# Transformer block, gate and up products: other signs, and two of four weight sums by an adding transfer

## The chip, the cores and the metric

The kernel runs on one core of one Trainium2 chip. The time is device microseconds of one execution. Engines are named as in the profile: PE (TensorE; PEld is its weight load), DVE (VectorE), ACT (ScalarE), POOL (GpSimd) and SP (SyncE, which here only issues DMAs).

## The reference

One encoder layer on 1024 positions of width 1024, all in float32. The change lies in the last part, the feed-forward network with 2816 hidden columns:

```
x = x + mix @ w_out                      # mix: convolution heads and neighbourhood attention
h = rms_norm(x, norm2_g)
x = x + (silu(h @ w_gate) * (h @ w_up)) @ w_down
```

## The kernel before

All matrix products are made in float32r with operands split in two: a high part (ACT's cast) and a low part (source minus high part, on DVE or POOL). Each product of tiles is three matmuls (L112 to L114: high by high, high by low, low by high). `split` at L103 does this splitting.

The gate and up products go by a Strassen-Winograd scheme with seven products in place of eight. The hidden columns are cut in 22 blocks of 128 (`FB`); block i has four weight quarters: gate and up, each for the first and second half of the 1024 inputs, named b11 (gate, first half), b21 (gate, second), b12 (up, first), b22 (up, second). The left operands are halves and sums of h, made once (A11, A12, A22, S1 to S4). The seven products of a block, m1 to m7, each take 4 x 3 matmuls of 128x512 and write to three PSUM banks A (m1, m2), B (m6, m5, m3) and D (m7, m4); a bank is accumulated on after DVE or ACT has read what stands in it. The order is m1, m6, m2, m5, m7, m3, m4 (`ORDER`), except that blocks 0 and 1 go through the products side by side.

Weights come by SP in two loads of 512 KB per block (`load_gu`, L874, three buffers `R`). Four weight sums per block are made on DVE (`t_sums`, L882, tiles ts): T1 = b12 - b11, T2 = b22 - T1, T3 = b22 - b12, T4 = b21 - T2. Each of the seven weight tiles (three quarters, four sums) is then split by ACT and POOL to a tile t (t9m in the profile is any of block 9's seven). Tiles ts, t and the results g come from one pool of 22 buffers (`G`).

Two functions set the order, both written out by hand. `product(i, p)` issues the matmuls, `evac(i, p)` the reading of a bank (L1025 to L1047: L1028 for m6, L1033 for m5, L1035 for m7, L1037 for m3, L1041 for m4). After each, `prep` issues the next task: the split of the weight tile of a product that comes four later, with the sums and loads that belong to it (L898 to L926). So sums, splits, evacuations and loads stand in one program order per engine, and each engine works through its own in order. An evacuated block is stored to DRAM (`keep`, L1052, sd), with sums of pairs of blocks on DVE (L1067), for the down projection that follows. While block 0 and 1 run, transposes and splits of the left operands (`s_T`, L946) are woven between their matmuls; S4 is the last of them, split on DVE.

Of the kernel before, what the change touches and what calls it, by code (L numbers as in the profile page):

```python
# [21 lines left out]
FB = FF // P  # L22
# [8 lines left out]
def layout(v):  # L31
    f = {k: np.asarray(a)[0] for k, a in v.items()}
    w_in = f["w_in"]
    ag = w_in[:, :2 * DC].reshape(KB, P, 8, P).transpose(2, 1, 0, 3)
    qkv = w_in[:, 2 * DC:].reshape(4, 2, P, 3, 512).transpose(3, 0, 2, 1, 4)
    gu = np.stack([f["w_gate"], f["w_up"]]).reshape(2, KB, P, FB, P).transpose(3, 0, 2, 1, 4)
    wd = f["w_down"].reshape(FB, P, D)
    par = np.concatenate([
        f["norm1_g"].reshape(KB, P).T,
        f["dw_kernel"].reshape(CW, 4, P).transpose(2, 1, 0).reshape(P, 4 * CW),  # L40
        f["dw_bias"].reshape(4, P).T,
        f["conv_ln_g"].reshape(4, P).T,
        f["conv_ln_b"].reshape(4, P).T,
        np.concatenate([f["q_norm_g"]] * 2)[:, None],
        np.concatenate([f["k_norm_g"]] * 2)[:, None],
    ], axis=1)
    out = {
        "x": f["x"],
        "xt": f["x"].T.reshape(4, 2, P, 2, 512).transpose(3, 0, 2, 1, 4),
        "ag": ag.reshape(8, P, KB * P),  # L50
        "qkv": qkv.reshape(3, 4, P, 1024),
        "wo": f["w_out"],
        "gu": gu.reshape(FB, 2, P, KB * P),
        "wd": wd,
        "g2": f["norm2_g"][None],
        "rpb": f["rpb"],
        "par": par,
    }
    return {k: np.ascontiguousarray(a) for k, a in out.items()}
# [8 lines left out]
def build(ctx, tc, a):  # L68
    nc = tc.nc
    pe, act, dve, pool = nc.tensor, nc.scalar, nc.vector, nc.gpsimd  # L70
# [26 lines left out]
    def tp(name):  # L97
        return ps.tile([P, 512], F32, tag="tp", bufs=2, name=name)

    def cv(name):  # L100
        return ps.tile([P, 1024], F32, tag="cv", bufs=1, name=name)

    def split(hi, lo, src, sub=(pool,)):  # L103
        act.copy(hi, src)  # L104
        n = src.shape[-1] // len(sub)
        for i, eng in enumerate(sub):
            sl = slice(i * n, (i + 1) * n)
            eng.tensor_tensor(*[w[..., sl] for w in (lo, src, hi.bitcast(F32))], OP.subtract)  # L108
# [397 lines left out]
    for kp in range(4):  # L506
# [13 lines left out]
        for j in range(2):  # L520
            for t in range(2):
                k = 2 * kp + j
# [175 lines left out]
    s1 = score_mm(1)  # L698
# [173 lines left out]
    raw_gu, top, tsum = {}, {}, {}  # L872

    def load_gu(i, j):  # L874
        if i < FB:
            raw_gu[i, j] = R(f"gu{i}{j}")
            nc.sync.dma_start(raw_gu[i, j], a["gu"][ms[i], j])

    def lr(w):
        return w[:, :512], w[:, 512:]  # L880

    def t_sums(i, ns):  # L882
        (b11, b21), (b12, b22) = lr(raw_gu[i, 0]), lr(raw_gu[i, 1])
        for n in ns:
            if n in (1, 3):
                tsum[i, n // 2] = G(f"ts{i}{n}")
            o = lr(tsum[i, (n - 1) // 2])[(n - 1) % 2]
            l, r = ((b12, b11), (b22, lr(tsum[i, 0])[0]), (b22, b12), (b21, lr(tsum[i, 0])[1]))[n - 1]
            dve.tensor_tensor(o, l, r, OP.subtract)  # L889


    ORDER = ("m1", "m6", "m2", "m5", "m7", "m3", "m4")
    ms = [m + h * QF for m in range(QF) for h in range(2)]
# [4 lines left out]
    def prep(n=1):  # L898
        for _ in range(n):
            if not tasks:  # L900
                return
            i, p = tasks.pop(0)
            if i < 2:
                if i == 1 and p in ("m6", "m5"):
                    t_sums(i, (1, 2) if p == "m6" else (3, 4))
            elif p == "m1":
                t_sums(i, (1, 2))
            elif p == "m6":
                t_sums(i, (3, 4))
            b = {"m1": (0, 0), "m2": (0, 1), "m3": (1, 1)}.get(p)  # L910
            n = {"m5": 0, "m6": 1, "m7": 2, "m4": 3}.get(p)
            src = lr(raw_gu[i, b[0]])[b[1]] if b else lr(tsum[i, n // 2])[n % 2]
            top[i, p] = lr(G(f"t{i}{p}", F32R))
            split(*top[i, p], src, (dve,) if i < 2 and p in ("m1", "m2", "m6", "m5") else (pool,))
            if (i, p) == (0, "m2"):
                load_gu(1, 1)
            if (i, p) == (1, "m5"):
                load_gu(2, 0)
            if (i, p) == (0, "m3"):
                load_gu(2, 1)  # L920
            if (i, p) == (1, "m3"):
                load_gu(3, 0)
            if i > 1 and p == "m2":
                load_gu(i + 1, 1)
            if i > 1 and p == "m3":
                load_gu(i + 2, 0)  # L926
# [3 lines left out]
    sn, sop = {}, {}  # L930

    def s_sum(t, ns, eng):
        (x11, x12), (x21, x22) = lr(xn[t]), lr(xn[t + 4])
        for n in ns:
            if n == 1:
                sn[t] = G(f"sn{t}")
            s1, s2 = lr(sn[t])
            o, l, r, op = ((s1, x21, x22, OP.add), (s2, s1, x11, OP.subtract),
                           (x21, x11, x21, OP.subtract), (x12, x12, s2, OP.subtract))[n - 1]
            eng.tensor_tensor(o, l, r, op)  # L940

    def s_rows(n, t):
        return {"S1": lambda: sn[t][:, :512], "S2": lambda: sn[t][:, 512:], "S3": lambda: xn[t + 4][:, :512],
# [2 lines left out]
    def s_T(n, kb):  # L946
        if kb == 0:
            if n == "S4":
                q = [lr(G(f"S4{i}", F32R)) for i in range(HK)]
                sop[n] = [[w[h] for w in q] for h in range(2)]  # L950
            else:
                q = H(n, F32R).rearrange("p (w k s) -> p w k s", w=2, s=512)
                sop[n] = [[q[:, h, i] for i in range(HK)] for h in range(2)]
                sop[n, "all"] = [q[:, h] for h in range(2)]
        two = kb == 2
        pt = cv("sp") if two else tp("sq")
        for j in range(1 + two):
            for t in range(4):
                pe.transpose(pt[:, j * 512 + t * P:j * 512 + (t + 1) * P],
                             s_rows(n, t)[:, (kb + j) * P:(kb + j + 1) * P], ident)  # L960
        if two and n != "S4":
            split(*[w[:, kb:kb + 2].rearrange("p k s -> p (k s)") for w in sop[n, "all"]], pt, (dve,))
        else:
            for j in range(1 + two):
                split(sop[n][0][kb + j], sop[n][1][kb + j], lr(pt)[j] if two else pt, (dve,))
# [41 lines left out]
    gt, bank, sl, u2, late = {}, {}, {}, {}, []  # L1007
# [12 lines left out]
    def evac(i, p, acc):  # L1020
        if p == "m1":
            gt[i] = G(f"g{i}")
        l, r = lr(gt[i])
        if p == "m1":
            (act.copy if i else dve.tensor_copy)(l, acc)  # L1025
        elif p == "m6":
            u2[i] = ST(f"u2{i}")
            dve.tensor_tensor(u2[i], acc, l, OP.add)  # L1028
        elif p == "m2":
            sl[i] = ST(f"sl{i}") if i < 2 else acc  # L1030
            act.activation(sl[i], acc, AF.Silu)  # L1031
        elif p == "m5":
            dve.tensor_tensor(r, acc, l, OP.add)  # L1033
        elif p == "m7":
            dve.tensor_tensor(r, acc, r, OP.add)  # L1035
        elif p == "m3":
            dve.tensor_tensor(l, acc, l, OP.add)  # L1037
            dve.tensor_tensor(l, sl[i], l, OP.mult)
            keep(i, 0, l)
        else:  # L1040
            dve.tensor_tensor(acc, acc, u2[i], OP.add)  # L1041
            act.activation(acc, acc, AF.Silu)  # L1042

            def f():
                dve.tensor_tensor(r, acc, r, OP.mult)
                keep(i, 1, r)
            late.append(f)  # L1047
# [165 lines left out]
    for s, p in enumerate(SEQ):  # L1213
        for k in range(QF - 2):
            n = s * QF + k
# [34 lines left out]
```

## Time and profile before

| | us |
|---|---|
| median of 3 runs | 1069.12 (1068.72 to 1070.26) |
| span of the profiled execution | 1067.6 |
| PE busy | 1047.3 (98%) |
| DVE busy | 701.1 (66%) |
| ACT busy | 451.0 (42%) |
| POOL busy | 381.1 (36%) |

The span runs from the first to the last instruction of the profiled execution; the runs' times are of whole executions, 1.1 to 2.7 us longer, and the profiled execution's own time is not listed beside its span. Matmuls overlap, so a matmul of 0.39 us is followed by the next one after 0.23 us. DMA-issuing instructions are not counted as busy on their engines. In the timelines a row is start, us taken, engine, line, operation, output<-inputs, and in brackets the idle time before it and who ended it. The gate and up stage runs from about 420 to 845 us, the down projection from there to the end.

### The profile page before, as it was taken

Reading aid. Unit: us, or ns where it says so; the run is one execution under the profiler, and the core shown is the slowest. Engines: PE = TensorE matmul, PEld = TensorE weight load, DVE = VectorE, ACT = ScalarE, POOL = GpSimd, SP = SyncE. Lnnn points to the kernel's source line nnn. Section 1 sums busy time; section 2 is a strip of 40 time slices with the busy share of each in tenths; the row PEclk is TensorE's granted clock in tenths of the full one; section 3 lists DMA queues with packets and bytes.
Section 4 is the critical chain, followed back from the end, with each engine's and each line's share of the span. In section 5 each row is a group of like instructions: output and inputs, shape, how many; then the busy total and the mean of one; then the engine's idle time right before and its main releaser. Section 6 shows DMA issues by size and latency. Waiting matters only on the chain.

```text
span 1067.6 us, 14069 instructions
## 1 busy us (share of the span) xinstructions
PE 1047.3 (98%) x5068; PEld 848.8 (80%) x5068; DVE 701.1 (66%) x1071; ACT 451.0 (42%) x987; POOL 381.1 (36%) x301
## 2 busy tenths in 40 slices
PE   7999999989999999999999999999999999999997
PEld 5888888866667888788888888888888888888886
DVE  6768997895775346766556465564655567858873
ACT  6465357725775424542322323223232344433441
POOL 0126675513562301445444554445554300002310
PEclk9999999989999999999999999999999999999999
DMA  8416781234414522132322322333232597634641
GB/s 328 167 48 223 218 247 53 75 141 147 152 61 126 163 86 80 41 117 81 128 99 91 128 99 89 109 111 111 74 129 79 184 328 276 207 99 128 206 128 41
DMA packets 68245, 144.06 MB, mean 135 GB/s; under 512 B 12496, under 2 KB 21200, under 8 KB 67536
## 3 DMA queue, kind: packets, MB, share of 16 engines
q1 hardware_dynamic: 66336, 139.95, 39.1%
q10 hardware_dynamic: 1840, 3.22, 0.9%
q8 instruction: 40, 0.66, 0.2%
q14 instruction: 29, 0.24, 0.1%
HBM read 103.99 MB, written 44.76 MB: 139 GB/s over the span
## 4 chain that ended last, share of the span: by engine, by line
PE 94%; DVE 4%; ACT 1%; DMA 0%; issue 0%; SPq 0%; ACTq 0%; DVEq 0%
PE B L114 6%; PE B L112 6%; PE B L113 6%; PE A L112 4%; PE D L114 4%; PE D L112 4%; PE A L114 4%; PE D L113 4%; PE A L113 4%; PE z L112 3%; PE z L113 3%; PE z L114 3%; DVE cv L319 3%; PE gl L114 3%; PE gl L112 3%; PE gl L113 3%
## 5 line engine op out<-in xcount | busy, mean ns | idle before, releaser
L319 DVE SCALAR_TENSOR_TENSOR cv<-u,par,cv 128x1009 f32<-128x1009 f32 (+14 forms) x92 | 117.5, 1277 | 2.5
L345 POOL TENSOR_TENSOR pa<-pa,pr 128x1022 f32<-128x1022 f32 (+5 forms) x24 | 57.5, 2396 | 50.3 <-ACT pr L344 41.9
L104 ACT CAST op<-sr 128x512 fp32r<-128x512 f32 x77 | 47.7, 619 | 51.5 <-PE B2d L114 23.4
L1033 DVE TENSOR_TENSOR g<-B,g 128x512 f32<-128x512 f32 x22 | 15.2, 690 | 78.9 <-PE B L114 78.9
L108 DVE TENSOR_TENSOR op<-sr,op 128x512 fp32r<-128x512 f32 x77 | 56.4, 732 | 16.1 <-ACT op L104 15.8
L1205 POOL TENSOR_TENSOR ou<-ou,resm 128x512 f32<-128x512 f32 x8 | 12.1, 1522 | 144.1 <-DMA resm<-xd 142.2
L1042 ACT ACTIVATE D<-D 128x512 f32<-128x512 f32 x22 | 12.8, 582 | 113.1 <-DVE D L1041 113.1
L1028 DVE TENSOR_TENSOR u<-B,g 128x512 f32<-128x512 f32 x22 | 15.2, 691 | 62.5 <-PE B L114 62.5
L104 ACT CAST op<-wd 128x512 fp32r<-128x512 f32 x66 | 40.9, 620 | 31.4 <-DVE wd L1120 18.1
L633 POOL TENSOR_SCALAR e<-e,rs 128x288 f32<-128x288 f32 (+1 forms) x64 | 34.1, 545 | 51.9 <-DVE rs L631 42.4
L108 DVE TENSOR_TENSOR op<-wd,op 128x512 fp32r<-128x512 f32 x66 | 50.3, 763 | 2.6 <-ACT op L104 1.1
L889 DVE TENSOR_TENSOR ts<-gu,ts 128x512 f32<-128x512 f32 x44 | 51.0, 1159 | 0.8
L1031 ACT ACTIVATE A<-A 128x512 f32<-128x512 f32 x20 | 11.6, 582 | 76.3 <-PE A L114 76.3
L626 ACT ACTIVATE e<-e,mx 128x288 f32<-128x288 f32 (+1 forms) x64 | 36.2, 569 | 11.4 <-DVE mx L624 11.4
L889 DVE TENSOR_TENSOR ts<-gu 128x512 f32<-128x512 f32 x22 | 34.1, 1550 | 0.0
L624 DVE CUSTOM_DVE_ANT_0 e<-s,tab 128x288 f32<-128x288 f32 (+1 forms) x64 | 30.0, 504 | 5.7 <-PE s L611 5.4
L611 PE MATMUL s<-kT,qT 64*128 64x288 f32 (+1 forms) x128 | 28.1, 499 | 4.6 <-DVE mx L624 4.6
L642 PEld LDWEIGHTS p<-ident,e 128*96 128x96 f32 (+1 forms) x192 | 20.1, 133 | 15.0 <-issue 10.4
L372 ACT ACTIVATE sq<-z,r 128x64 f32<-128x64 f32 x96 | 28.6, 334 | 2.2 <-PE z L114 2.2
L642 PE MATMUL p<-ident,e 128*96 128x128 f32 (+1 forms) x192 | 27.6, 280 | 0.6 <-DVE pT L647 0.6
L658 PE MATMUL o<-pT,vw 96*64 96x128 f32 (+1 forms) x384 | 28.0, 281 | 0.0
L344 ACT ACTIVATE pr<-u,par 128x1022 f32<-128x1022 f32 (+5 forms) x24 | 27.0, 1138 | 1.6 <-ACT vs L403 1.6
(1039 smaller groups left out, 3451.4 us busy)
## 6 DMA issues: line engine op xcount, KB each, us to landing
gu<-in_gu SPq DMA_DIRECT2D x44, 512.0 KB
sr<-sd SPq DMA_DIRECT2D x77, 256.0 KB
sd<-sd SPq DMA_DIRECT2D x22, 512.0 KB
wd<-in_wd SPq DMA_DIRECT2D x44, 256.0 KB
sd<-g SPq DMA_DIRECT2D x33, 256.0 KB
x<-in_x SPq DMA_DIRECT2D x16, 512.0 KB
xd<-x SPq DMA_DIRECT2D x8, 512.0 KB
resm<-xd SPq DMA_DIRECT2D x16, 256.0 KB
```

The costliest lines, as they stand in the source:

```text
L104: act.copy(hi, src)
L108: eng.tensor_tensor(*[w[..., sl] for w in (lo, src, hi.bitcast(F32))], OP.subtract)
L112: pe.matmul(acc, lh, rh, start=start, stop=False, skip_group_check=True)
L113: pe.matmul(acc, lh, rl, start=False, stop=False, skip_group_check=True)
L114: pe.matmul(acc, ll, rh, start=False, stop=stop, skip_group_check=True)
L319: dve.scalar_tensor_tensor(acc[:, o], uc[:, i], dwk[:, c, t:t + 1], acc[:, o], OP.mult, OP.add)
L345: pool.tensor_tensor(pa[:, o], pa[:, o], pr[:, o], OP.add)
L624: dve.tensor_tensor_reduce(out=e[:, hh], in0=ss[hh], in1=tab[rh, cb][2 * hp + hh], scale=-1.0, scalar=3.0e38, op0=OP.add, op1=OP.min, accu ...
L626: act.activation(e[:, hh], e[:, hh], AF.Exp, bias=mx, scale=-1.0, accum_out=rs[:, hh:hh + 1])
L633: pool.tensor_scalar(es[i][:, hh], es[i][:, hh], rs[:, hh:hh + 1], 1.0, op0=OP.mult, op1=OP.mult)
L642: pe.transpose(pt[:m, g * P:(g + 1) * P], es[i][:, hh, g * m:(g + 1) * m], ident)
L889: dve.tensor_tensor(o, l, r, OP.subtract)
```

## The change

The signs of the operands are chosen so that all four weight sums are additions: P1 = b11 + b12, P2 = P1 + b22, P3 = b12 + b22, P4 = P2 + b21. The evacuations, the Silu of m4 (scale -1) and the left operands (S1, S2, S3, A22) take the opposite signs where needed. In DRAM the weight quarters are paired anew: the first load of a block is (b11, b22), the second (b12, b21).

For the blocks from 2 on, P1 and P3 lie in one tile of 128x1024 and are no longer made on DVE. `t_first` has SP load b12 into both halves of the tile (two loads of 256 KB), one block ahead, at the split of m1. `t_add` has POOL issue one transfer of 512 KB that adds (b11, b22) from DRAM to the tile, one block ahead, after the split of m7; for block 2 both stand at the splits of m3 of blocks 0 and 1, and for block 3 the loads stand at the split of m1 of block 2. DVE makes P2 at the split of m1 and P4 at the split of m6. Blocks 0 and 1 make all four sums on DVE.

```diff
+    def t_first(i):
+        if i < FB:
+            tsum[i, 0] = G(f"ts{i}0")
+            for j in range(2):
+                nc.sync.dma_start(lr(tsum[i, 0])[j], a["gu"][ms[i], 1][:, :512])
+
+    def t_add(i):
+        if i < FB:
+            pool.dma_start(tsum[i, 0], a["gu"][ms[i], 0], accum_op=OP.add)
+
     def t_sums(i, ns):
-        (b11, b21), (b12, b22) = lr(raw_gu[i, 0]), lr(raw_gu[i, 1])
+        (b11, b22), (b12, b21) = lr(raw_gu[i, 0]), lr(raw_gu[i, 1])
         for n in ns:
-            if n in (1, 3):
-                tsum[i, n // 2] = G(f"ts{i}{n}")
-            o = lr(tsum[i, (n - 1) // 2])[(n - 1) % 2]
-            l, r = ((b12, b11), (b22, lr(tsum[i, 0])[0]), (b22, b12), (b21, lr(tsum[i, 0])[1]))[n - 1]
-            dve.tensor_tensor(o, l, r, OP.subtract)
+            if (n, i < 2) in ((1, True), (2, False)) or n == 2:
+                tsum[i, n - 1] = G(f"ts{i}{n}")
+            if n in (1, 3) and i > 1:
+                continue
+            (p1, p3), (p2, p4) = lr(tsum[i, 0]), lr(tsum[i, 1]) if (i, 1) in tsum else (None, None)
+            o, l, r = ((p1, b11, b12), (p2, p1, b22), (p3, b12, b22), (p4, p2, b21))[n - 1]
+            dve.tensor_tensor(o, l, r, OP.add)
...
             if (i, p) == (0, "m3"):
                 load_gu(2, 1)
+                t_first(2)
             if (i, p) == (1, "m3"):
                 load_gu(3, 0)
+                t_add(2)
+            if i > 1 and p == "m1":
+                t_first(i + 1)
+            if i > 1 and p == "m7":
+                t_add(i + 1)
...
-        if two and n != "S4":
+        if n == "A22":
+            w = slice(kb, kb + 1 + two)
+            hi, lo = [q[:, w].rearrange("p k s -> p (k s)") for q in sop[n, "all"]]
+            act.activation(hi, pt, AF.Copy, scale=-1.0)
+            dve.scalar_tensor_tensor(lo, pt, -1.0, hi.bitcast(F32), OP.mult, OP.subtract)
+        elif two and n != "S4":
...
         elif p == "m6":
             u2[i] = ST(f"u2{i}")
-            dve.tensor_tensor(u2[i], acc, l, OP.add)
+            dve.tensor_tensor(u2[i], acc, l, OP.subtract)
...
             dve.tensor_tensor(acc, acc, u2[i], OP.add)
-            act.activation(acc, acc, AF.Silu)
+            act.activation(acc, acc, AF.Silu, scale=-1.0)
```

DVE in block 9, before. The rows go from the evacuation of m6 to that of m3; ts101 and ts103 are the sums of block 10, gu100 and gu101 its loads, g9 the result, B9 and D9 the banks:

```order
L1028 TENSOR_TENSOR u29_5432<-B9_5419,g9_5413 128x512
L1033 TENSOR_TENSOR g9_5413<-B9_5419,g9_5413 128x512
L889 TENSOR_TENSOR ts101_5468<-gu101_5381,gu100_5301 128x512
L889 TENSOR_TENSOR ts101_5468<-gu101_5381,ts101_5468 128x512
L1035 TENSOR_TENSOR g9_5413<-D9_5474,g9_5413 128x512
L889 TENSOR_TENSOR ts103_5488<-gu101_5381 128x512
L889 TENSOR_TENSOR ts103_5488<-gu100_5301,ts101_5468 128x512
L1037 TENSOR_TENSOR g9_5413<-B9_5419,g9_5413 128x512
```

The same place on DVE in the changed kernel (its lines are numbered anew: L1056 is the evacuation of m5, L1058 of m7, L1060 of m3); ts100 is the tile that the adding transfer fills:

```order
L1051 TENSOR_TENSOR u29_5444<-B9_5431,g9_5424 128x512
L1056 TENSOR_TENSOR g9_5424<-B9_5431,g9_5424 128x512
L902 TENSOR_TENSOR ts102_5480<-ts100_5351,gu100_5312 128x512
L1058 TENSOR_TENSOR g9_5424<-D9_5488,g9_5424 128x512
L902 TENSOR_TENSOR ts102_5480<-ts102_5480,gu101_5392 128x512
L1060 TENSOR_TENSOR g9_5424<-B9_5431,g9_5424 128x512
```

Two sums are gone, and the one ahead of the evacuation of m7 now reads a tile that transfers have filled.

POOL in block 9, before: the splits of m5, m7, m3 and m4.

```order
L108 TENSOR_TENSOR t9m5_5397<-ts91_5335,t9m5_5397 128x512
L108 TENSOR_TENSOR t9m7_5416<-ts93_5357,t9m7_5416 128x512
L108 TENSOR_TENSOR t9m3_5434<-gu91_5241,t9m3_5434 128x512
L108 TENSOR_TENSOR t9m4_5452<-ts93_5357,t9m4_5452 128x512
L108 TENSOR_TENSOR t10m1_5471<-gu100_5301,t10m1_5471 128x512
```

The same place on POOL in the changed kernel:

```order
L109 TENSOR_TENSOR t9m5_5408<-ts90_5212,t9m5_5408 128x512
L109 TENSOR_TENSOR t9m7_5427<-ts90_5212,t9m7_5427 128x512
L891 DMA ts100_5351<-in_gu 128x1024
L109 TENSOR_TENSOR t9m3_5446<-gu90_5176,t9m3_5446 128x512
L109 TENSOR_TENSOR t9m4_5464<-ts92_5346,t9m4_5464 128x512
L109 TENSOR_TENSOR t10m1_5482<-gu100_5312,t10m1_5482 128x512
```

The adding transfer for block 10 (L891) stands between the splits of m7 and m3 of block 9. On SP, where the stage begins, the changed kernel has these rows (gu21 is the second load of block 2, gu30 the first of block 3, L887 the two loads of `t_first`):

```order
L878 DMA gu20_4203<-in_gu 128x1024
L878 DMA gu21_4304<-in_gu 128x1024
L887 DMA ts20_4306<-in_gu 128x512 x2
L878 DMA gu30_4338<-in_gu 128x1024
L887 DMA ts30_4378<-in_gu 128x512 x2
```

Before, the three loads gu20, gu21 and gu30 stood there one behind the other; the loads for the tiles ts20 and ts30 have come between and behind them.

More of the change, by code (lines that the diff above doesn't have):

```diff
@@ L35, in layout @@
     qkv = w_in[:, 2 * DC:].reshape(4, 2, P, 3, 512).transpose(3, 0, 2, 1, 4)
-    gu = np.stack([f["w_gate"], f["w_up"]]).reshape(2, KB, P, FB, P).transpose(3, 0, 2, 1, 4)
+    gu = np.stack([f["w_gate"], f["w_up"]]).reshape(2, 2, KB // 2, P, FB, P).transpose(4, 0, 1, 3, 2, 5)
+    gu = np.stack([np.stack([gu[:, 0, 0], gu[:, 1, 1]], 2), np.stack([gu[:, 1, 0], gu[:, 0, 1]], 2)], 1)
     wd = f["w_down"].reshape(FB, P, D)
@@ L909, in prep @@
                 t_sums(i, (3, 4))
-            b = {"m1": (0, 0), "m2": (0, 1), "m3": (1, 1)}.get(p)
-            n = {"m5": 0, "m6": 1, "m7": 2, "m4": 3}.get(p)
-            src = lr(raw_gu[i, b[0]])[b[1]] if b else lr(tsum[i, n // 2])[n % 2]
+            b = {"m1": (0, 0), "m2": (1, 1), "m3": (0, 1)}.get(p)
+            n = {"m5": (0, 0), "m6": (1, 0), "m7": (0, 1), "m4": (1, 1)}.get(p)
+            src = lr(raw_gu[i, b[0]])[b[1]] if b else lr(tsum[i, n[0]])[n[1]]
             top[i, p] = lr(G(f"t{i}{p}", F32R))
@@ L937, in s_sum @@
             s1, s2 = lr(sn[t])
-            o, l, r, op = ((s1, x21, x22, OP.add), (s2, s1, x11, OP.subtract),
-                           (x21, x11, x21, OP.subtract), (x12, x12, s2, OP.subtract))[n - 1]
-            eng.tensor_tensor(o, l, r, op)
+            o, l, r = ((s1, x21, x22), (s2, x11, s1), (x21, x21, x11), (x12, x12, s2))[n - 1]
+            eng.tensor_tensor(o, l, r, OP.subtract)
     def s_rows(n, t):
@@ L1032, in evac @@
         elif p == "m5":
-            dve.tensor_tensor(r, acc, l, OP.add)
+            dve.tensor_tensor(r, acc, l, OP.subtract)
         elif p == "m7":
@@ L1036, in evac @@
         elif p == "m3":
-            dve.tensor_tensor(l, acc, l, OP.add)
+            dve.tensor_tensor(l, acc, l, OP.subtract)
             dve.tensor_tensor(l, sl[i], l, OP.mult)
```

## The prediction

> **What bounds the kernel now.** I read the page's first two parts, then the table of busy time by stretches, then the waits of PE, and only then the timelines of the engines that the change touches. The page:
>
> ```profile
> span 1067.6 us, 14069 instructions
> PE 1047.3 (98%) x5068; PEld 848.8 (80%) x5068; DVE 701.1 (66%) x1071; ACT 451.0 (42%) x987; POOL 381.1 (36%) x301
> PE 94%; DVE 4%; ACT 1%; DMA 0%; issue 0%; SPq 0%; ACTq 0%; DVEq 0%
> ```
>
> PE is busy for 98% of the span and carries 94% of the chain that ended last. Whether the 98% is even is seen in the stretches (us of the stretch, then PE, PEld, DVE, ACT, POOL busy, granted clock, DMA share, GB/s). Gate and up run from about 420 to 845 us:
>
> ```profile
> 390.00:430.00 40.00, 39.34 (x189) 31.95 (x188) 26.34 (x40) 16.86 (x33) 5.19 (x3) 1.00 0.24 93
> 430.00:470.00 40.00, 39.58 (x212) 32.34 (x212) 28.15 (x40) 20.34 (x34) 17.64 (x14) 1.00 0.12 40
> 470.00:510.00 40.00, 40.00 (x178) 33.13 (x177) 24.56 (x31) 10.52 (x20) 20.23 (x15) 1.00 0.32 112
> ...
> 790.00:830.00 40.00, 40.00 (x178) 33.14 (x177) 23.53 (x29) 11.19 (x21) 20.95 (x16) 1.00 0.27 96
> sum 360.00, PE 360.00 PEld 298.10 DVE 205.87 ACT 103.34 POOL 180.97; mean PE 40.00 PEld 33.12 DVE 22.87 ACT 11.48 POOL 20.11
> ```
>
> From 470 to 830 us PE is busy 360 of 360 us at full clock. In the 80 us before, it lacks 0.66 + 0.42 = 1.1 us. The waits of PE say the same (us in total, times, longest); after 400 us there are two rows:
>
> ```profile
> PE t L990 <- DVE xn L863: 0.6, 1, 0.6
> PE B L113 <- DVE S L108: 0.3, 1, 0.3
> ```
>
> So in the stage that is changed, PE waits for nothing. VectorE is busy only 206 of 360 us there and has no share in the time.
>
> **What is removed.** For the 20 blocks from the third on, two of four sums on DVE go. The groups of the sums, by shape:
>
> ```profile
> L889 DVE TENSOR_TENSOR ts<-gu,gu 128x512 f32<-128x512 f32 x22 | 16.8, 762 | 0.0
> L889 DVE TENSOR_TENSOR ts<-gu 128x512 f32<-128x512 f32 x22 | 34.1, 1550 | 0.0
> ```
>
> 20 x 762 ns + 20 x 1550 ns = 46 us of DVE. PE did not wait for them, so their worth is 0; at most the 1.1 us above could come back, and nothing in it hangs on these sums. The other signs (subtract for add, Silu and Copy with scale -1, the A22 split as one scalar_tensor_tensor) exchange instructions one for one on the same shapes: 0.
>
> **What is added in steady state.** Per block SP issues two more 256 KB loads, and Pool one 512 KB transfer that adds: 20 x 1 MiB = 21 MB beside 144 MB, at a DMA share near 0.3. The question is when the adding transfer lands, because DVE's sum p2 waits for it, and DVE works in order. Take blocks 8 and 9 (tiles t8m, t9m), where the transfers for blocks 9 and 10 are issued. The first line is the page's total, the others are of the timelines of Pool, DVE and PE (start, us taken):
>
> ```profile
> DMA packets 68245, 144.06 MB, mean 135 GB/s; under 512 B 12496, under 2 KB 21200, under 8 KB 67536
> 588.70 1.29 POOL L108 TENSOR_TENSOR t8m<-ts,t8m 128x512 fp32r<-128x512 f32 x1 [0.70 <-ACT t8m L104]
> ...
> 606.38 2.65 POOL L108 TENSOR_TENSOR t9m<-ts,t9m 128x512 fp32r<-128x512 f32 x2 [3.77 <-ACT t9m L104]
> 608.98 1.31 POOL L108 TENSOR_TENSOR t9m<-gu,t9m 128x512 fp32r<-128x512 f32 x1
> 614.79 0.69 DVE L1033 TENSOR_TENSOR g<-B,g 128x512 f32<-128x512 f32 x1 [4.75 <-PE B L114]
> 617.44 0.69 DVE L1035 TENSOR_TENSOR g<-D,g 128x512 f32<-128x512 f32 x1 [0.43 <-PE D L114]
> 600.92 0.39 PE L112 MATMUL D<-A,t8m 128*128 128x512 f32 x1
> ...
> 619.96 0.39 PE L112 MATMUL D<-A,t9m 128*128 128x512 f32 x1
> ```
>
> In block 9 Pool ends the splits of m5 and m7 at 609.03; there the transfer is issued. DVE comes to the sum at 614.79 + 0.69 = 615.5. Queued behind it is L1035, the evacuation of m7, and for that PE waits: m4 accumulates on the same bank D from 619.96. With 0.69 for the sum and 0.69 for L1035, the transfer must land by 619.96 - 1.38 = 618.6, that is 9.5 us after its issue. (In block 8 the split of m7 ends at 588.70 + 1.29 and PE comes to D at 600.92: also 9.5.) A later landing costs PE its lateness once per block, for 19 blocks.
>
> The trace has no Pool transfer and no addition. The nearest rows are two plain transfers of 512 KB from SP:
>
> ```profile
> 591.27 0.33 SPq L877 DMA_DIRECT2D gu<-in_gu  x1
> 592.70 0.33 SPq L1069 DMA_DIRECT2D sd<-sd  x1
> 590.00:592.00 2.00, 2.00 (x10) 1.65 (x9) 1.31 (x3) 0.00 (x0) 1.25 (x1) 1.00 0.01 4
> 592.25:595.50 3.25, 3.25 (x16) 2.67 (x16) 0.42 (x1) 1.62 (x3) 1.36 (x2) 1.00 0.86 320
> ```
>
> Data flow 1.0 us after SP's issue, and 1 MB takes 3.25 us, 1.6 us for each 512 KB. Issue to data on Pool: between 1.0 (as SP) and 3.25 (as long as that whole MB); I take 1.9, the nearer to SP's, since it is the same kind of command. Duration: between 1.6 (a plain transfer) and four times that, 6.5 (a choice, as no row bounds it); I take 3.25, two plain transfers, because out += in has to read both sides. Pool held by the command: between 0.3 (SP's issue) and 3.25 again; I take 1.3, one split. Then data start at 610.9. Pool's split for m3 ends at 611.6 instead of 610.3, it frees the slot for which SP waits, and SP's load and the two new loads (1 MB, 3.25 us) start at 612.6. Until then 1.7 us of the addition are done; the other 1.55 share the engines half and half and take 3.1: it lands at 615.7. That is 0.2 us after DVE is ready and 2.9 us before PE would notice. Steady state: 0. Hold of Pool: a block takes PE 619.96 - 600.92 = 19.04 us, one of its seven products 2.72; m3, the product before m4, starts at 617.2 and is split by 610.3 today, so a hold of up to 6.9 us is hidden.
>
> **What is added at the start.** For block 2 the loads and the addition are asked for one after the other, in the last tasks of blocks 0 and 1:
>
> ```profile
> 454.63 1.28 POOL L108 TENSOR_TENSOR t0m<-gu,t0m 128x512 fp32r<-128x512 f32 x1 [0.96 <-ACT t0m L104]
> 457.33 1.30 POOL L108 TENSOR_TENSOR t1m<-gu,t1m 128x512 fp32r<-128x512 f32 x1 [0.17 <-ACT t1m L104]
> 458.66 0.33 SPq L877 DMA_DIRECT2D gu<-in_gu  x1
> 456.75:459.00 2.25, 2.25 (x14) 1.86 (x13) 1.82 (x2) 0.57 (x2) 1.72 (x2) 1.00 0.66 233
> 462.04 0.69 DVE L1041 TENSOR_TENSOR D<-D,u 128x512 f32<-128x512 f32 x1
> 464.39 0.69 DVE L108 TENSOR_TENSOR S<-sp,S 128x512 fp32r<-128x512 f32 x1 [0.34 <-ACT S L104]
> 465.73 0.69 DVE L108 TENSOR_TENSOR S<-sp,S 128x512 fp32r<-128x512 f32 x1 [0.65 <-ACT S L104]
> 467.18 0.39 PE L113 MATMUL B<-S,t0m 128*128 128x512 f32 x1
> ```
>
> SP's load for block 2 is released by Pool at 455.9 and its data end by 459.0. The new plain loads follow it: 459.0 + 1.6 = 460.6. Pool, free at 458.6, waits for them and issues the addition at 460.6; data from 462.5. On the engines then is what SP issued from 458.66 on (1 MB, 460.6 to 463.85): 1.35 us of it is left, shared until 465.2; the last 1.9 us of the addition run alone: landing at 467.1. DVE has been ready since 462.73. Behind its sum stand two splits of S4, 2.03 us from the start of the first to the end of the second (464.39 to 466.42), and PE needs the second at 467.18. So the landing may not be later than 467.18 - 2.03 - 0.69 = 464.46, and 467.1 costs PE 2.6 us, once. With the low bounds (issue to data 1.0, duration 1.6) it lands at 464.9 and costs 0.4; with the duration of four plain transfers it costs 5.9.
>
> **Sum.** 1067.6 - 0 + 0 + 2.6 = 1070.2 us of span. The span is 1.5 us below the runs' median of 1069.12 (the profiled execution's own time around its span is not listed apart), so I predict 1071.7 us.
>
> At this place the Trainium skill has a price, "DMA: Bandwidth & Descriptors", section "Anatomy of one DMA — SWDGE (gpsimd) path": 2.0 us plus bytes over 436 GB/s for a transfer issued from GpSimd, an estimate of 3.2 us for 512 KB. By it the addition lands at 612.2 in steady state and at 463.8 at the start, and the sum is 1069.1; but it is a plain transfer's price, and the same page of the Trainium skill, under "Rules for kernel authors", says that an accumulating transfer reads its destination and writes it later, which speaks against this change. No run so far shows either.
>
> **The rivals.**
>
> *The addition is slow.* Above 2.9 plain transfers (4.7 us alone) it misses 618.6: 1.7 us done before 612.6, 3.0 shared after. At four (6.5 us): 1.7 + 3.25 until 619.1, the last 1.55 alone, landing 620.65, 2.05 us late x 19 = 39 us, with 5.9 at the start 1114 us; at five, 3.6 x 19 + 7.5 = 76 us, 1145. For it: each transfer shares the engines with 1 MB from SP, and nothing in the trace prices an addition. Against it: a margin of 2.9 us, and SP's traffic ends by itself. Chance 0.30.
>
> *Hidden at the start too; not slower.* Loads and addition come at plain prices, landing at 464.9 or before: 1069.1 to 1069.5. For it: nothing but the nearest row. Against: two streams are read. The Trainium skill's fit above would give this case. Chance 0.17.
>
> *DVE's relief reaches PE; faster.* It would need PE waits that end in DVE; the two rows above hold 0.9 us, and PE lacks 1.1 us in all, so 1068.0, which is within 0.2%. More than 2 us would need a PE pace that no row shows. Chance 0.05 for over 0.2%.
>
> *The change does not do what it says,* or Pool is held over 6.9 us per command: each us more costs 19 us. DVE has 40 fewer instructions, so the first part is out. Chance 0.03.
>
> **How the numbers follow.** The forecast (steady state hidden, start 1 to 4 us) has 0.45, and its own range is 1070 to 1073.1. A measurement of this kernel can tell about 0.2%, 2.1 us, from no change, so a loss over 2.1 counts as slower: of the 0.45, 0.27 slower and 0.18 the same. Slower: 0.27 + 0.30 + 0.03 = 0.60; same: 0.18 + 0.17 = 0.35; faster 0.05. The range begins at 1068.0, the hidden case less the 1.1 us that PE lacks, and ends at 1114, an addition of four plain transfers; beyond lie a good part of the slow case and most of the faster one, 0.2 together.
>
> **What would show it.** Right: PE 40.00 of 40 us from 470 on; 2 to 3 us of a PE wait on DVE S at 466 to 469 us, and one DVE wait there on the adding transfer; in steady state DVE's sum p2 waits under 1 us. Wrong: PE waits for DVE at bank D (L1058) in every block, or Pool idle before the split of m3 while PE waits for it. A PE wait for the tile t of m6 or m5 would mean that I missed a dependency.

## The result and the profile after

The changed kernel takes 1075.27 us (median; 1074.97 to 1075.85), the kernel before 1069.18 in the same comparison: ratio 1.0054, 95% interval 1.0042 to 1.0066, a loss of 6.1 us. The forecast was a loss of 2.6 us, 1071.7, in the range 1068.0 to 1114. The page after, its totals:

```profile
span 1074.1 us, 14260 instructions
PE 1050.6 (98%) x5068; PEld 850.4 (79%) x5068; DVE 670.1 (62%) x1031; ACT 451.3 (42%) x987; POOL 396.1 (37%) x321
PE 90%; DVE 5%; ACT 1%; issue 1%; DMA 1%; POOL 0%; SPq 0%; POOLq 0%; ACTq 0%; DVEq 0%
DMA packets 76889, 165.06 MB, mean 154 GB/s; under 512 B 13457, under 2 KB 22161, under 8 KB 76177
```

DVE's busy time fell by 31 us and DMA gained 21 MB. In the chain, PE gave 4% of the span to others. The same stretches as before (columns as there) tell where:

```profile
430.00:470.00 40.00, 35.79 (x194) 28.86 (x192) 22.50 (x32) 17.22 (x29) 16.70 (x13) 0.99 0.27 79
470.00:510.00 40.00, 39.62 (x162) 32.28 (x163) 20.94 (x27) 12.61 (x23) 20.86 (x17) 0.92 0.51 158
510.00:550.00 40.00, 40.00 (x178) 33.11 (x177) 19.52 (x24) 11.00 (x21) 22.41 (x18) 1.00 0.50 152
...
790.00:830.00 40.00, 40.00 (x178) 33.14 (x177) 18.77 (x23) 12.62 (x23) 21.07 (x17) 1.00 0.56 162
```

From 510 us on nothing has changed for PE: 40.00 of 40 us, 178 matmuls per stretch, granted clock 1.00. Two stretches differ from before. From 430 to 470 PE lacks 4.2 us instead of 0.4. From 470 to 510 it is busy 39.62 us but ends only 162 matmuls, at a mean granted clock of 0.92 (the share of full speed that the profile records for PE): the matmuls themselves are slower. The waits of PE (us in total, times, longest):

```profile
PE z L113 <- ACT wk0h L105: 6.6, 1, 6.6
PE B L114 <- DVE S L109: 4.5, 2, 4.2
```

The second row was 0.3 before. The first, the wait for the first weights, was 7.4 before; over the profiled runs of this study it lay between 6.2 and 8.0, whatever the kernel. The place in the timelines (start, us taken, operation, idle time before and its releaser), of SP, Pool, DVE and PE in this order:

```profile
445.31 10.49 SPq L878 DMA_DIRECT2D gu<-in_gu  x2
455.89 0.86 SPq L887 DMA_DIRECT2D ts<-in_gu  x2
458.61 0.86 SPq L887 DMA_DIRECT2D ts<-in_gu  x2
456.86 1.30 POOL L109 TENSOR_TENSOR t1m<-gu,t1m 128x512 fp32r<-128x512 f32 x1 [0.17 <-ACT t1m L105]
461.37 1.02 POOL L891 DMA_DIRECT2D ts<-in_gu  x1 [3.21 <-PE D L115]
469.03 0.69 DVE L902 TENSOR_TENSOR ts<-ts,gu 128x512 f32<-128x512 f32 x1 [6.83 <-issue]
469.64 0.68 DVE L109 TENSOR_TENSOR S<-sp,S 128x512 fp32r<-128x512 f32 x1
465.81 0.39 PE L113 MATMUL B<-S,t0m 128*128 128x512 f32 x1
470.38 0.79 PE L114 MATMUL B<-S,t0m 128*128 128x512 f32 x1 [4.18 <-DVE S L109]
472.79 0.63 PE L113 MATMUL B<-S,t1m 128*128 128x512 f32 x1
473.22 0.63 PE L114 MATMUL B<-S,t1m 128*128 128x512 f32 x1
477.15 0.40 PE L113 MATMUL A<-h,t2m 128*128 128x512 f32 x1
```

SP's command for gu21 stands 10.49 us in the queue (with gu20's), waiting for a raw buffer; the plain loads for block 2 are issued at 455.89, behind it. Pool is free at 458.2, waits 3.2 us and issues the addition at 461.37. (The profile names a matmul as its releaser; the program's wait there is for the two plain loads.) DVE has waited 6.83 us when the p2 sum starts at 469.03, so the addition landed about 7.6 us after its issue. The S4 split is queued behind the sum, and PE stands 4.18 us for it. The matmuls that follow start 0.43 us apart instead of 0.23. The stretches here, cut where the granted clock changes:

```profile
465.99:469.40 3.41, 0.20 (x1) 0.00 (x0) 0.37 (x1) 0.00 (x0) 0.00 (x0) 1.00 0.18 34
469.40:472.81 3.41, 2.43 (x6) 1.64 (x7) 2.70 (x5) 1.03 (x2) 0.00 (x0) 0.50 0.00 0
472.81:476.23 3.42, 3.42 (x10) 2.68 (x9) 3.01 (x4) 1.69 (x4) 2.69 (x2) 0.50 0.01 2
476.23:479.64 3.41, 3.41 (x16) 2.81 (x15) 1.98 (x3) 0.00 (x0) 1.52 (x2) 1.00 0.63 232
```

The granted clock goes to 0.50 at 469.4, still within the pause, and stays there for 6.83 us, two stretches of 3.41. A measure that takes both together: from the first matmul of m3 of block 0 (B<-S,t0m) to the first of m1 of block 2 (A<-h,t2m) lie 24 matmuls. That took 5.45 us before (464.91 to 470.36) and 12.71 us after (464.44 to 477.15): 7.26 us lost, 4.2 in the pause and 3.1 behind it, at half clock. Less the 0.8 us by which the first wait was shorter in this execution, that is the 6.5 us between the two spans. Below, "lost" is this stretch less 5.45 us.

### The profile page after: what moved, and what is told of

Read it like the earlier page. It is cut to its first block, busy times and chain, and to the rows that moved or that the text cites. A ratio compares the mean times of both kernels' runs of the same rounds, so it can differ in the third digit from the quotient of the medians.

```text
span 1074.1 us, 14260 instructions
## 1 busy us (share of the span) xinstructions
PE 1050.6 (98%) x5068; PEld 850.4 (79%) x5068; DVE 670.1 (62%) x1031; ACT 451.3 (42%) x987; POOL 396.1 (37%) x321
## 3 DMA queue, kind: packets, MB, share of 16 engines
q0 software_dynamic: 2880, 10.49, 5.7%
## 4 chain that ended last, share of the span: by engine, by line
PE 90%; DVE 5%; ACT 1%; issue 1%; DMA 1%; POOL 0%; SPq 0%; POOLq 0%; ACTq 0%; DVEq 0%
PE B L114 6%; PE B L115 6%; PE B L113 6%; PE A L113 4%; PE A L115 4%; PE A L114 4%; PE D L113 3%; PE D L115 3%; PE D L114 3%; PE z L113 3%; PE z L114 3%; PE z L115 3%; DVE cv L320 3%; PE gl L115 3%; PE gl L113 3%; PE gl L114 3%
## 5 line engine op out<-in xcount | busy, mean ns | idle before, releaser
L1056 DVE TENSOR_TENSOR g<-B,g 128x512 f32<-128x512 f32 x22 | 15.2, 691 | 69.6 <-PE B L115 69.6
L902 DVE TENSOR_TENSOR ts<-ts,gu 128x512 f32<-128x512 f32 x44 | 43.9, 998 | 6.9 <-issue 6.8
L958 POOL TENSOR_TENSOR xn<-xn,xn 128x512 f32<-128x512 f32 x4 | 6.9, 1734 | 57.5 <-DVE sn L958 57.5
```

The lines of the kernel that those rows point to most:

```text
L902: dve.tensor_tensor(o, l, r, OP.add)
```

## The experiments

**Is it the start alone, and which part of it?** Four versions in one comparison (the kernel before: 1069.42 us). The first makes block 2's sums on VectorE.

```diff
-            if (n, i < 2) in ((1, True), (2, False)) or n == 2:
+            if (n, i < 3) in ((1, True), (2, False)) or n == 2:
...
-            if n in (1, 3) and i > 1:
+            if n in (1, 3) and i > 2:
...
-                t_first(2)
...
-                t_add(2)
```

> All four weight sums of block 2 are made on VectorE, as those of blocks 0 and 1 are; the transfers with addition begin with block 3. Theory (the loss is one stall at the start: the transfer for block 2 lands late, VectorE's in-order queue holds the S4 splits behind the p2 sum, TensorE stands 4.2 us, and its granted clock is 0.50 for 6.8 us after it): both go, 1068.7 to 1069.7 us. Rival 'signs' (the new signs cost some 0.3 us in each block): still 1075. Rival 'twenty transfers' (each of the 20 costs some 0.3 us through the load on the DMA engines): 19 of 20 stay, 1074.7 to 1075.2.

1070.33 us, ratio 1.0010 (1.0001 to 1.0019). The loss falls from 6.1 to 0.9 us with 19 of the 20 additions in place; lost: 0.0. What the 0.9 is, the trace doesn't show; it is within the 0.2% that a measurement can tell. The second leaves the transfer and moves the sum:

```diff
-            elif p == "m1":
+            elif p == "m1" and i > 2:
                 t_sums(i, (1, 2))
             elif p == "m6":
-                t_sums(i, (3, 4))
+                t_sums(i, (3, 4) if i > 2 else (1, 2, 3, 4))
```

> The transfer of block 2 is issued where it was and lands as late as before (about 469.0 us), but the p2 sum of block 2 stands on VectorE behind the last two S4 splits and the m4 evacuation of block 1, beside the p4 sum. Theory (it isn't the late landing that costs, but what stands behind the waiting sum on VectorE): TensorE runs through m3 of blocks 0 and 1 and m1 of block 2, which takes it to some 472.5 us, and the split of p2 is done by about 471.6 to 472.5: stall 0 to 1 us, no drop of the clock, 1068.7 to 1070.2 us. Rival 'late data' (block 2 needs the sum so soon that TensorE stands for it wherever the sum is queued): 1073 to 1075.

1069.93 us, 1.0007 (0.9998 to 1.0016), lost 0.0. Its timelines of Pool and DVE:

```profile
463.39 1.02 POOL L891 DMA_DIRECT2D ts<-in_gu  x1 [3.25 <-PE D L115]
465.84 0.69 DVE L109 TENSOR_TENSOR S<-sp,S 128x512 fp32r<-128x512 f32 x1 [1.66 <-ACT S L105]
467.19 0.69 DVE L109 TENSOR_TENSOR S<-sp,S 128x512 fp32r<-128x512 f32 x1 [0.65 <-ACT S L105]
469.33 1.42 DVE L902 TENSOR_TENSOR ts<-ts,gu 128x512 f32<-128x512 f32 x2 [0.84 <-issue]
```

All of this execution lies 2 us later (its first wait was 8.0). Here PE began m3 of block 0 at 466.42, so the addition lands 2.9 us after that (in the changed kernel 4.6: the landing took 7.6 us there and 5.9 here); in its old place the sum would have had to start within 0.4 us of it (the 1.35 us from its start to PE's restart, against PE's stop at 466.2, and 464.44 for m3, in the changed kernel). DVE still waits 0.84 us for the landing, but both S4 splits have gone ahead and PE waits for nothing. So a landing 2.5 us too late for the old place costs only through what is queued behind it. The third issues the loads and the addition earlier:

```diff
             if (i, p) == (0, "m3"):
+                t_first(2)
                 load_gu(2, 1)
-                t_first(2)
+                t_add(2)
             if (i, p) == (1, "m3"):
                 load_gu(3, 0)
-                t_add(2)
```

> Block 2's two plain loads are issued ahead of its second weight load, and its transfer with addition one task earlier on GpSimd, behind the m3 split of block 0. Theory: the plain loads no longer queue on SyncE behind the weight load that waits for a raw buffer, so the transfer is issued at about 455.5 instead of 461.4 us and lands by 461 to 463, before VectorE reaches the p2 sum at 462.2 or within 1 us of it; no stall, 1068.7 to 1069.7 us. Rival 'twenty transfers' (steady state costs): still 1073 to 1075. A gain over the kernel before (under 1068.5) would show that the 46 us of work taken from VectorE reach TensorE somewhere; I expect none.

1069.84 us, 1.0004 (0.9995 to 1.0013), lost 0.0. Pool and DVE, and the sum of the nine stretches from 470 to 830 us:

```profile
456.83 1.01 POOL L891 DMA_DIRECT2D ts<-in_gu  x1
463.86 0.69 DVE L902 TENSOR_TENSOR ts<-ts,gu 128x512 f32<-128x512 f32 x1 [0.21 <-issue]
sum 360.00, PE 360.00 PEld 298.20 DVE 174.82 ACT 103.48 POOL 195.81; mean PE 40.00 PEld 33.13 DVE 19.42 ACT 11.50 POOL 21.76
```

The landing is a tie with DVE (0.21 us), though 6.9 us after the issue. With all 20 additions at work PE is busy 360 of 360 us; DVE carries 175 us there instead of 206, and the time is that of the kernel before. The fourth keeps the signs and the layout and makes every sum on VectorE:

```diff
-            if (n, i < 2) in ((1, True), (2, False)) or n == 2:
+            if n < 3:
                 tsum[i, n - 1] = G(f"ts{i}{n}")
-            if n in (1, 3) and i > 1:
-                continue
...
-                t_first(2)
...
-                t_add(2)
-            if i > 1 and p == "m1":
-                t_first(i + 1)
-            if i > 1 and p == "m7":
-                t_add(i + 1)
```

> The new signs and the new layout of the weights stay, but all four sums of every block are additions on VectorE; there are no plain second loads and no transfers with addition. Theory: the signs cost nothing, 1068.7 to 1069.7 us. Rival 'signs': 1073 to 1075, with TensorE waiting on the negated evacuations.

1069.46 us, 1.0001 (0.9992 to 1.0009). The signs cost nothing. Taking two of four sums from DVE (the third version against the fourth) brings nothing either.

**What makes the first landing late?** Three versions (the kernel before: 1069.15, for the second 1069.12). First only the plain loads go ahead:

```diff
             if (i, p) == (0, "m3"):
+                t_first(2)
                 load_gu(2, 1)
-                t_first(2)
```

> Only block 2's two plain loads are moved: ahead of its second weight load on SyncE. The transfer with addition stays where it is on GpSimd, behind the m3 split of block 1. Theory: GpSimd's idle 3.2 us ahead of that transfer was the wait for the plain loads, so it is now issued at about 458.2 us; with 5.6 to 7.6 us to landing it lands at 463.8 to 465.8. VectorE can take the sum as late as about 464.85 (the sum's start lay 1.35 us ahead of TensorE's restart in the changed kernel, and TensorE would go on at 466.2): a stall of 0 to 1.6 us, and no drop of the clock if that needs a long pause: 1068.8 to 1071.0 us. Rival 'any pause drops the clock': 1072 to 1074.5.

1074.15 us (1072.53 to 1074.58), 1.0043 (1.0030 to 1.0055): a miss. The profiled execution, the 1072.53, has on Pool and DVE, and as landings of the 20 additions:

```profile
459.07 1.00 POOL L891 DMA_DIRECT2D ts<-in_gu  x1
467.58 0.69 DVE L902 TENSOR_TENSOR ts<-ts,gu 128x512 f32<-128x512 f32 x1 [4.41 <-issue]
DMA to landing us min/median/max: 5.4/5.6/8.4
```

Pool's 3.2 us of idle time are gone, as expected, but the landing took 8.4 us: SP now issues the second weight load of block 2, the first of block 3 and block 3's plain loads within 4 us of it. The pause was 1.77 us, the clock stayed at 1.00, lost 2.8. Why the other executions were 1 to 2 us longer the one profile doesn't show; by the record the mean granted clock was lower in two of the four (0.993 and 0.994 against 0.996), so it may have fallen there; in the other two it was the same as in the profiled one. The next version moves block 3's plain loads away from the addition:

```diff
-            if i > 1 and p == "m1":
+            if i > 1 and p == ("m1" if i > 2 else "m5"):
                 t_first(i + 1)
```

> The changed kernel with one thing moved: block 3's two plain loads are issued three tasks later on SyncE, so that they no longer run beside block 2's transfer with addition. Theory 'the transfer lands late because it shares the DMA engines with plain loads' (5.6 us from issue to landing in the median, 7.6 and 8.4 us at the start, where other loads were under way): it is issued at 461.4 as before and lands after 5.6 to 6.5 us, at 467.0 to 467.9; TensorE pauses 2.1 to 3.1 us instead of 4.2: 1071.5 to 1072.5 us if the clock holds, 1073 to 1075 if it falls. Rival 'the first transfer of its queue is slow whatever runs beside it': 7.6 us to landing and 1075 us as before.

Its landings, the pause on PE, and the stretches behind it:

```profile
DMA to landing us min/median/max: 5.4/5.6/5.8
468.59 0.50 PE L114 MATMUL B<-S,t0m 128*128 128x512 f32 x1 [1.97 <-DVE S L109]
470.00:472.00 2.00, 2.00 (x6) 1.60 (x7) 1.97 (x4) 1.48 (x3) 0.30 (x1) 0.67 0.00 0
472.00:474.00 2.00, 2.00 (x6) 1.58 (x5) 2.00 (x2) 0.66 (x2) 2.00 (x2) 0.50 0.00 0
474.00:476.00 2.00, 2.00 (x10) 1.62 (x10) 1.07 (x3) 0.00 (x0) 1.94 (x2) 0.97 0.51 170
```

No landing takes over 5.8 us, so the 2 us too many came with the loads beside it. But these loads don't always cost as much: in the second version of the first comparison SP issues the same loads as close (block 3's plain loads at 460.55, the addition at 463.39; in the changed kernel 458.61 and 461.37), and there the landing took 5.9 us. In the changed kernel the last 2 us of the landing were a tail at 25 GB/s and an eighth of the DMA engines' time:

```profile
466.50:468.50 2.00, 0.00 (x0) 0.00 (x0) 0.00 (x0) 0.00 (x0) 0.00 (x0) 1.00 0.13 25
```

What decides whether there is such a tail the runs don't show. In the version above the pause falls to 1.97 us; the clock falls all the same, for 3.4 us, and the time is 1074.26 us, 1.0048 (1.0034 to 1.0062). The third version leaves the addition out, so that P1 and P3 hold weights and no sums:

```diff
-            pool.dma_start(tsum[i, 0], a["gu"][ms[i], 0], accum_op=OP.add)
+            pool.dma_start(tsum[i, 0], a["gu"][ms[i], 0])
```

> Leaves the addition out: the same transfers on GpSimd's queue, at the same places and of the same size, overwrite the tile that the two plain loads filled, so that P1 and P3 hold weights and no sums. It tells how much of the landing time is the addition. Theory (the addition moves its bytes at about half the rate of a plain load, 3.3 against 1.6 us for 512 KB): median landing falls from 5.6 to about 4 us; at the start it lands 1.6 us or more sooner, at about 467, and the stall falls to 2.6 us or less: 1071.5 to 1072.5 if the clock holds, 1074 to 1075 if it still drops. Rival 'the queue costs, not the addition': landing stays 5.6 us, time stays 1075.

```profile
DMA to landing us min/median/max: 3.6/3.8/4.0
```

1071.61 us, 1.0024 (1.0015 to 1.0033). A plain transfer on the same queue lands in 3.8 us in the median, the addition takes 5.6: 1.8 us more for 512 KB. The pause is 0.66 us, the clock stays at 1.00.

**What does a pause of PE cost by itself?** The kernel before, with the first sum of block 2 repeated on VectorE, so that DVE is late there and no transfer is involved (11, 8 and 5 repeats, the edit shown for 8; the kernel before: 1069.15, for five repeats 1069.12):

```diff
-            dve.tensor_tensor(o, l, r, OP.subtract)
+            for _ in range(9 if (i, n) == (2, 1) else 1):
+                dve.tensor_tensor(o, l, r, OP.subtract)
```

> The kernel before, with the first sum of block 2 made nine times instead of once (eight repeats, 0.61 us each, into the same tile): no transfer with addition anywhere, VectorE alone is late at the place where the changed kernel is late. It tells what a pause of TensorE costs by itself. The last S4 splits come 4.9 us later; TensorE would need the first of them 2.0 us after its old end: pause 2.9 us and 0.65 us more behind it for the next split. Theory 'clock falls after a long pause': at 2.9 us it is open whether it falls: 1072.0 to 1073.0 if it holds at 1.00, 1074.5 to 1075.5 if it is 0.50 for 6.8 us (3.2 us of matmul lost, which hides the 0.65). Rival 'the clock has nothing to do with the pause': 1072.0 to 1073.0, here and by the same sum 1074 to 1075 at eleven repeats.

> The kernel before, with the first sum of block 2 made twelve times instead of once (eleven repeats of 0.61 us): pause of TensorE 4.7 us, a little longer than the 4.2 us of the changed kernel. Theory 'clock falls after a long pause': 0.50 for 6.8 us behind it, 3.2 us more, 1069.2 + 4.7 + 3.2 = 1077 us. Rival 'the clock has nothing to do with the pause': 1074 to 1075.

> The kernel before, with the first sum of block 2 made six times instead of once. A repeat delayed TensorE by 0.73 us in the runs with eight and eleven repeats (pauses of 4.87 and 7.05 us), so five repeats give a pause of 2.7 us, the size that the prediction gave the stall. Theory 'the clock falls only when most of a window of 3.41 us is without matmuls': pauses of 1.77 us left it at 1.00, pauses of 4.2 us and over brought it to 0.50; at 2.7 us it is open. If it holds: 1069.2 + 2.7 - 0.3 (the wait that was there) + 0.3 = 1071.9 us, 1071.5 to 1072.5. If it falls for 3.41 us 1.6 us more, for 6.8 us 3.2 us more: 1073.5 to 1075.3. Rival 'the clock has nothing to do with it': 1071.9 and 1.00 throughout.

A repeat took 0.8 us, not 0.61, so the pauses came out longer than planned: 4.87 us at eight repeats (1077.04 us, 1.0074, 1.0060 to 1.0088) and 7.05 at eleven (1079.01, 1.0090, 1.0076 to 1.0104). Both brought the clock down. Five repeats gave 2.7 us, about the 2.6 that the prediction had put on the stall; PE, and the stretches behind:

```profile
469.12 0.50 PE L113 MATMUL B<-S,t0m 128*128 128x512 f32 x1 [2.69 <-DVE S L108]
470.00:472.00 2.00, 1.77 (x5) 1.25 (x5) 2.00 (x4) 0.95 (x2) 0.00 (x0) 0.57 0.00 0
472.00:474.00 2.00, 2.00 (x7) 1.57 (x6) 1.97 (x4) 1.19 (x3) 1.77 (x2) 0.58 0.00 0
```

1074.67 us, 1.0051 (1.0039 to 1.0064): 5.5 us for a pause of 2.7. Last, the changed kernel with the pause filled by work that nobody uses (the kernel before: 1069.76):

```diff
+            if (i, p, k) == (0, "m3", 2):
+                fill = tp("fill")
+                for n in range(16):
+                    pe.matmul(fill, th[:, :P], s[0][0], start=n == 0, stop=n == 15, skip_group_check=True)
             mac(acc, [q[:, k * P:(k + 1) * P] for q in (th, tl)], [s[h][k] for h in range(2)],
```

> The changed kernel, late transfer and all, with 16 extra matmuls (a scratch bank that nobody reads) on TensorE directly ahead of the product step that has to wait for the S4 split. At 0.23 us each they take 3.7 us of the 4.2 us pause, so TensorE goes on at the same moment as in the changed kernel, but has had work until shortly before. Theory 'the pause takes the granted clock to 0.50': the clock stays at 1.00, the 3.2 us of half-speed matmul go, the pause itself stays: 1075.3 - 3.2 = 1072.1 us, 1071.6 to 1073.3 (0.65 us may come for the next split, which half speed hid). Rival 'the half clock has another cause, or the lost time isn't the clock': 1074.8 to 1075.8.

```profile
466.49 3.79 PE L1041 MATMUL fill<-S,t0m 128*128 128x512 f32 x16
470.64 0.50 PE L114 MATMUL B<-S,t0m 128*128 128x512 f32 x1
470.00:472.00 2.00, 1.68 (x6) 0.56 (x4) 1.29 (x3) 0.59 (x1) 0.00 (x0) 1.00 0.00 0
472.00:474.00 2.00, 1.95 (x9) 1.63 (x10) 1.97 (x4) 1.37 (x3) 0.18 (x1) 1.00 0.00 0
```

The addition is nearly as late (7.2 us after its issue) and PE's own work goes on nearly as late (5.5 us after the start of m3 instead of 5.9), but the clock stays at 1.00: it was the lack of matmuls that brought it down. 1073.96 us, 1.0040 (1.0027 to 1.0054), above the 1071.6 to 1073.3 expected. In the trace 4.76 us are lost instead of 7.26; of the 3.2 us expected, 2.5 came, and 0.4 of these by the earlier landing; at full speed PE waits for the next split instead. In the times the two intervals overlap, so there the gain is not certain.

The runs together (pause: the longest wait on the S4 splits; half clock: how long the granted clock was 0.50 behind it; lost: as defined above; all from one profiled execution):

| version | pause | half clock | lost | median less before |
|---|---|---|---|---|
| plain transfer | 0.66 | 0 | 1.67 | 2.5 |
| plain loads ahead | 1.77 | 0 | 2.78 | 5.0 (3.4 in this execution) |
| block 3's loads later | 1.97 | 3.4 | 4.51 | 5.1 |
| five repeats | 2.69 | 3.4 | 5.14 | 5.5 |
| the changed kernel | 4.18 | 6.8 | 7.26 | 6.1 |
| the same, filled | 0.3 | 0 | 4.76 | 4.2 |
| eight repeats | 4.87 | 3.4 | 6.66 | 7.9 |
| eleven repeats | 7.05 | 6.8 | 9.34 | 9.9 |

With the clock at 1.00 throughout (the first two rows) 1.0 us more is lost than the pause, as PE then has to wait for the next S4 split too. Slower matmuls hide that wait. So of the 3.1 us that the changed kernel loses behind its pause, the clock added about 2.1, which is also what the filled version gained beyond its earlier landing (2.5 less 0.4).

**How much slack had the steady state?** (The kernel before: 1069.12.) With block 2 mended as in the third version above, each addition is issued two tasks later:

```diff
-            if i > 1 and p == "m7":
+            if i > 1 and p == "m4":
                 t_add(i + 1)
```

> Block 2 as in the version with its loads and its addition issued early; in the steady state each transfer with addition is issued two tasks later on GpSimd, behind the split of m4 instead of m7. It measures the slack that the steady state had. In block 9 of the changed kernel the transfer was issued at 615.77 us, GpSimd's m4 split ended at 621.27, and VectorE's m7 evacuation, which stands behind the p2 sum, must be done when TensorE starts m4 at 626.96: p2 sum (0.69) and evacuation (0.69) take the latest landing to about 625.3. Theory (5.6 us to landing): issued at 621.3 it lands at 626.9, 1.6 us late, and TensorE waits 1.4 to 1.7 us in each of 19 blocks for VectorE: 1096 to 1102 us, the clock at 1.00. Rival 'there is more slack than I count': 1069 to 1075.

1120.15 us, 1.0476 (1.0452 to 1.0500). The landings, and PE's waits as block 5 and block 6 are begun (two of 19 such rows):

```profile
DMA to landing us min/median/max: 5.4/5.8/7.8
PE D L113 <- ACT t5m L105: 3.6, 1, 3.6
PE D L113 <- ACT t6m L105: 1.5, 1, 1.5
```

The waits on bank D are there in all 19 blocks: 1.2 to 1.5 us for the even blocks, a little under the 1.4 to 1.7 forecast, and 1.4 to 3.6 for the odd ones, where landings took up to 7.8 us. (The profile names ACT's cast of p2; it ends within 0.1 us of VectorE's evacuation, and both wait for the p2 sum.) They sum to 36.9 us. Behind eight of the ten odd ones the clock fell for 3.4 us, all but the two shortest, 1.4 and 1.6 us; behind no even one. Half clock for 3.4 us costs 1.6 (0.43 us a matmul instead of 0.23): 36.9 + 8 x 1.6 = 50, and 1069.8 + 50 = 1120, the median. The profiled execution, from which the waits are, took 1123.46, so 3 to 4 us of it stay unexplained. The expectation missed both the longer landings and the clock.

## Why the prediction was right, and where it was off

**PE is bound, DVE's relief (46 us by its groups, 31 in busy time) and the signs are worth 0: right.** Shown by the signs-only version (1.0001) and by the version with early loads (1.0004), both with 360 of 360 us on PE.

**Steady state 0: right, with more room than I gave it.** Block 10's addition and its sum in the changed kernel (Pool, then DVE), and the landings of all 20:

```profile
615.77 0.88 POOL L891 DMA_DIRECT2D ts<-in_gu  x1
621.57 0.69 DVE L1056 TENSOR_TENSOR g<-B,g 128x512 f32<-128x512 f32 x1 [4.73 <-PE B L115]
622.18 0.89 DVE L902 TENSOR_TENSOR ts<-ts,gu 128x512 f32<-128x512 f32 x1
DMA to landing us min/median/max: 5.4/5.6/7.6
```

The sum follows the evacuation without a wait. Landing took 5.6 us instead of 6.7, Pool was held 0.88 instead of 1.3. The addition's price, two plain transfers, was about right: 1.8 us over the plain one's 3.8, where the estimate was 1.65. The Trainium skill's fit ("DMA: Bandwidth & Descriptors", "Anatomy of one DMA — SWDGE (gpsimd) path"), an estimate of 3.2 us, is for a plain transfer; here that took 3.6 to 4.0, and nothing in the fit covers the addition. The slack of 9.5 us between issue and the latest landing was borne out by the even blocks of the last experiment, where an issue 5.5 us later made PE wait 1.2 to 1.5 us.

**The start, 2.6 us: the mechanism right, the term mis-sized; it measured 7.3.** The chain was the one forecast: plain loads late on SP, the addition behind them, DVE's p2 sum ahead of the S4 splits, one wait of PE on DVE S. Two things were wrong in its size. First the landing: 6.5 us from issue was assumed with the loads of block 3 beside it, 7.6 were measured (5.4 without them), and the issue came at 461.4 instead of 460.6 while PE ran 0.47 us earlier. With the 2.6 us forecast that makes 5.0 us at the second S4 split; 4.2 of it stood as a pause ahead of the first, the rest is hidden by the slower matmuls behind it. Second, and nearly as large, the step "costs PE its lateness" itself: here the granted clock was halved behind the pause, for 6.8 us, which makes up the rest of the 7.3, 2 us or a little more. Even the 2.6 us that I forecast would have cost about 5.5, as five repeats (2.7 us) show. The trace of before had the warning in it, which I did not use, behind its one wait of 4.6 us in the attention stage. The waits of PE, and the stretch (columns as above):

```profile
PE s L611 <- DVE mx L624: 4.6, 1, 4.6
236.00:238.00 2.00, 0.46 (x1) 0.46 (x2) 1.87 (x5) 0.42 (x1) 0.00 (x0) 0.50 0.00 0
```

**The chances.** The case that came (steady state hidden, the start not) was the likeliest, at 0.45; with the clock in the sum its price would have been 5 to 6 us, and most of that case slower; under a pause of 1.8 us the runs show no such price.

## What to carry to other kernels

Price a pause of the matmul engine not by its length alone: here behind a pause of 1.9 us or more the clock was halved for 3.4 or 6.8 us, which is 1.6 or 3.1 us of matmul time (about 2 of the 3.1 in the end in the changed kernel), so one long wait is worth more effort than several short ones. Before a transfer feeds an in-order engine, look at what is queued behind its first use and move that ahead; with the p2 sum two splits later, a transfer that was still 2.5 us too late for its old place cost nothing. And relief for an engine that the bound one never waits for was worth nothing here (46 us of it); the steady state was fine, and the first iteration, whose loads are asked for all at once, was where the change lost.

## What the runs showed of the hardware

Granted clock: by the trace's record it was 0.50 for 3.41 or 6.83 us after pauses of 1.88 us and more (13 of 13 in the gate and up stage of these profiles), and stayed at 1.00 after pauses of 0.66 to 1.77 us (13 of 13). The length of the pause doesn't set how long: 4.18 us brought 6.8, 4.87 us brought 3.4. The Trainium skill ("TensorE: Matmul & The Clock Gate", "What's actually happening") tells of a free-running window of 3413 ns; the steps of 3.41 and 6.83 us agree. It lets the clock fall after at least one idle window, about 3.4 us; here pauses of 1.9 to 2.7 us were enough, and the measurement decides.

The place of the pause accounts for both in these traces. All changes of the clock in one trace lie whole multiples of 3.41 us apart, so each trace can be cut into stretches of 3.41 us at these instants. In the gate and up stage the 13 stretches that end with a fall hold 1.54 to 3.41 us in which PE isn't busy, and no stretch after which the clock stayed at 1.00 holds more than 1.60. So what counts is the idle time within one such stretch, with the line at about 1.5 to 1.9 us. The clock came back after one stretch where that stretch held at most 0.28 us of idle PE (eight repeats: the pause of 4.87 us ends 0.28 us into it), and after two where it held 0.98 (the changed kernel) or 2.63 (eleven repeats). That is read from the traces; no run moved a pause on purpose. Nor is it the whole measure: behind the 4.6 us wait of the attention stage, where two matmuls of 64x288 come next, the clock was 0.50 for two stretches in every profile, also where PE was busy for 3.37 us of the first (the version with early loads).

An adding transfer of 512 KB from GpSimd landed after 5.4 to 5.9 us in the steady state of the changed kernel, where SP's next loads are issued 2.2 us or more behind it. For block 2, with 1 MB or more of plain loads issued in the 4 us ahead of it or beside it, it landed after 5.9 to 8.4, and in the odd blocks of the last experiment, which have such loads too, after 5.8 to 7.8.
